# Smaller first transfers, block-wise first products and another order of copies at the start of a macaron block

## The chip, the core and the metric

The kernel runs on one core of a Trainium2 chip. The core has a matrix engine (TensorE, PE in the profile; its weight loads are listed as PEld), VectorE (DVE), ScalarE (ACT), GpSimd (POOL) and SyncE (SP), each with its own instruction stream. They share an on-chip memory of 128 partitions, an accumulator memory in banks of 128 x 512 float32 that TensorE writes, and 16 DMA engines that move data to and from the device's main memory. A transfer is issued by an engine; nearly all of this kernel's are issued by SyncE, in the order of the program.

The metric is the time of one execution on the device in microseconds, the median of several runs.

## The reference

One layer of a decoder with 1024 tokens of width 1024, in float32: a half-step of a SwiGLU feed-forward, a mixer of two branches (dilated window attention and multi-scale pooling), a second half-step, and a final norm. Cut to what matters here:

```python
def rms_norm(x, g):
    xf = x.astype(jnp.float32)
    y = xf * lax.rsqrt(jnp.mean(xf * xf, axis=-1, keepdims=True) + RMS_EPS)
    return (y * g.astype(jnp.float32)).astype(x.dtype)

def swiglu(x, w1, w3, w2):
    return (jax.nn.silu(x @ w1) * (x @ w3)) @ w2

def reference(x, ffn1_norm, ffn1_w1, ffn1_w3, ffn1_w2, ...):
    h = x
    h = h + 0.5 * swiglu(rms_norm(h, ffn1_norm[0]), ffn1_w1[0], ffn1_w3[0], ffn1_w2[0])
    u = rms_norm(h, mix_norm[0])
    ...   # the mixer: h = h + merged @ w_out
    h = h + 0.5 * swiglu(rms_norm(h, ffn2_norm[0]), ffn2_w1[0], ffn2_w3[0], ffn2_w2[0])
    return rms_norm(h, final_norm)
```

The first half-step multiplies the normed x (1024 x 1024) by w1 and w3 (1024 x 2816 each). The change lies in the first few of these products.

## The kernel before

**Numbers.** A float32 operand is split into a rounded high part (made by ScalarE, `AF.Copy` into a type that TensorE multiplies in one pass) and a low part, the rest (made by VectorE or GpSimd as source minus high part). A product of two such operands is three matmuls: high by high, high by low, low by high (`three`). One *product* below is a 128-column piece of a weight over 512 rows of the contraction against 512 tokens: 4 blocks of 128 rows x 3 matmuls = 12 matmuls of 128 x 128 by 128 x 512.

**Seven products for eight.** The multiplications by w1 and w3 are done on 2 x 2 halves (contraction by tokens) with seven products in place of eight. The class `Quad` holds one 128-column piece of w1 (`a`) or w3 (`b`); quads 0 and 1 are `f10a` and `f10b`, quads 2 and 3 `f11a` and `f11b`, quads 4 and 5 `f12a` and `f12b`. Product m of a quad takes a weight operand and one of seven operands made of x:

- `b11` and `b21`: x of the first 512 tokens, rows 0 to 3 and 4 to 7 of the contraction in blocks of 128 (products 1 and 2).
- `b22`, and the sums `t2`, `t3`, `t1`, `t4` (products 3, 6, 7, 5 and 4).

`high(what, k, ...)` and `low(what, k, ...)` make the two parts of block k of such an operand; `operand(n, m)` makes the weight operand of product m of quad n (the high part on ScalarE, line 322; the low part on GpSimd or VectorE, line 325); `run(n, m)` issues the 12 matmuls (line 334), and `out(n, m)` takes the result from its bank. `led` products are product 1 of two later pairs, run ahead because x is still coming in: `led_high`, `led_run` and `led_out`, which copies the bank to the tile `s_f1led` and sends it to main memory.

**Order.** The stretch is written out by hand in the function `begin_up1` (`manual_schedule`): each engine does its instructions in the order in which the lines issue them, and waits on the others only for data and for places. `load_all` issues the transfers in one list on SyncE: x turned so that the contraction lies on partitions (`x_t`, two blocks of 128 rows in one transfer), the first halves of four weights (`raw0` to `raw3`), led weights, and then x by tokens (`row_x`), from which ScalarE takes the mean squares.

ffn1_norm (`gain1`) multiplies x while it is rounded (line 1057 the high part, line 1066 the low one). The root of the mean square is applied later, to the results: `squares_of_x`, `inverses`, `spread` (four transposes by `ident`, line 1115) and `spread_copy` put it into the tile `norm`.

**The first two products.** `run_first` issues them (line 1158) with the weights split in two pieces of 256 columns by `split_high` (ScalarE, line 1144) and `split_low` (GpSimd, line 1148). Thirteen small matmuls on a tile of ones (`idle`, line 1041) stand ahead of them.

## Time and profile before

| | |
|---|---|
| median of 3 runs | 1876.85 us (1876.06 to 1878.15) |
| profiled execution | 1876.94 us, its span 1874.9 us |
| TensorE busy | 1864.6 us (99%), 8690 matmuls |
| VectorE busy | 1369.0 us (73%) |
| ScalarE busy | 767.7 us (41%) |
| GpSimd busy | 782.5 us (42%) |
| first product's first matmul | 6.44 us after the span's start |
| granted TensorE clock, mean | 0.999 |

How to read it: times in a timeline count from the span's start. A timeline row is start, duration, engine, source line, operation, what it writes and reads with the buffer numbers left out, the shapes, the count, and in brackets how long the engine sat idle before it and what ended that. A row with x4 stands for four instructions in a row. The name `x_t` is x as loaded, `xhi_b_f` and `xlo_b_f` the parts of b11, b21 or b22, `xhi_t_f` and `xlo_t_f` those of a t operand, `wc_first` and `wc_f10a` and so on weight operands with both parts, `u_...` a bank, `y_f` and `u_f` results.

### The profile page before, as it was taken

What the parts mean: (1) busy time and instruction counts of PE and PEld (TensorE: products, weight loads), DVE (VectorE), ACT (ScalarE), POOL (GpSimd) and SP (SyncE); (2) the same over time, 40 slices, a digit from 0 to 9 for tenths busy, and PEclk for the clock granted to TensorE, in tenths of its full rate; (3) what the DMA queues carried; (4) which work ended last, traced back from release to release, by engine and by line L of the source; (5) the groups of instructions that cost most, each with busy time, mean ns of one, the idle gap of its engine ahead of it and who ended that gap; (6) DMA issues with size and microseconds to landing.
All of it is one profiled execution on the core that took longest, in us unless ns stands there. A gap on an engine that the chain in (4) does not pass through costs nothing.

```text
span 1874.9 us, 24458 instructions
## 1 busy us (share of the span) xinstructions
PE 1864.6 (99%) x8690; PEld 1546.4 (82%) x8690; DVE 1369.0 (73%) x1972; ACT 767.7 (41%) x1392; POOL 782.5 (42%) x566
## 2 busy tenths in 40 slices
PE   9999999999999999999999999999999999999998
PEld 7888888888888888888888888888888888888887
DVE  7887866668886776658885896888765566577867
ACT  8322323333345643334445762463333333334344
POOL 4554644452222364445554457544333333313221
PEclk9999999999999999999999999999999999999999
DMA  8134324356565435765678868734342233354654
GB/s 327 45 124 148 122 95 151 123 200 210 189 234 197 158 114 204 253 221 185 213 251 327 309 223 296 266 133 180 119 140 85 90 107 121 127 200 158 224 198 146
DMA packets 147473, 338.10 MB, mean 180 GB/s; under 512 B 17944, under 2 KB 39448, under 8 KB 145816
## 3 DMA queue, kind: packets, MB, share of 16 engines
q1 hardware_dynamic: 143608, 325.70, 50.3%
q10 hardware_dynamic: 3744, 10.85, 1.5%
q8 instruction: 68, 1.11, 0.3%
q14 instruction: 53, 0.43, 0.1%
HBM read 235.90 MB, written 100.60 MB: 179 GB/s over the span
## 4 chain that ended last, share of the span: by engine, by line
PE 54%; DVE 3%; ACT 2%; issue 1%; DMA 1%; POOL 1%; ACTq 0%; SPq 0%; DVEq 0%; POOLq 0%
PE u_mixm L334 15%; PE d_f L904 8%; PE wo L2345 4%; PE yp L2087 1%; PE u_f20a L334 1%; PE u_f21b L334 1%; PE u_f20b L334 1%; PE u_f21a L334 1%; PE u_f210b L334 1%; PE u_f210a L334 1%; PE u_f29b L334 1%; PE u_f29a L334 1%; PE u_f28b L334 1%; PE u_f28a L334 1%; PE u_f27b L334 1%
## 5 line engine op out<-in xcount | busy, mean ns | idle before, releaser
L904 PE MATMUL d_f<-bhi_f,ahi_f 128*128 128x512 f32 x616 | 240.2, 390 | 0.0
L904 PE MATMUL d_f<-bhi_f,alo_f 128*128 128x512 f32 x616 | 239.8, 389 | 0.0
L904 PE MATMUL d_f<-blo_f,ahi_f 128*128 128x512 f32 x616 | 239.6, 389 | 0.0
L861 POOL TENSOR_TENSOR alo_f<-g_f,ahi_f 128x512 fp32r<-128x512 f32 x60 | 89.6, 1511 | 266.2 <-ACT ahi_f L857 266.2
L334 PE MATMUL u_mixm<-xhi_t_mix,wc_mixm 128*128 128x512 f32 x608 | 157.3, 391 | 0.1
L904 PEld LDWEIGHTS d_f<-bhi_f,alo_f 128*128 128x128 f32 x616 | 115.6, 188 | 24.5 <-DVE alo_f L861 0.2
L904 PEld LDWEIGHTS d_f<-bhi_f,ahi_f 128*128 128x128 f32 x616 | 115.7, 188 | 24.2 <-ACT h L424 0.5
L904 PEld LDWEIGHTS d_f<-blo_f,ahi_f 128*128 128x128 f32 x616 | 115.7, 188 | 23.7
L334 PEld LDWEIGHTS u_mixm<-xhi_t_mix,wc_mixm 128*128 128x128 f32 x608 | 113.5, 188 | 23.8 <-ACT wc_mixm L322 0.6
L334 PE MATMUL u_mixm<-xhi_b_mix,wc_mixm 128*128 128x512 f32 x456 | 120.3, 391 | 0.0
L325 POOL TENSOR_TENSOR wc_mixm<-s_mixm,wc_mixm 128x512 fp32r<-128x512 f32 x52 | 77.9, 1499 | 99.1 <-ACT wc_mixm L322 88.2
L334 PEld LDWEIGHTS u_mixm<-xhi_b_mix,wc_mixm 128*128 128x128 f32 x456 | 85.0, 188 | 17.2
L322 ACT ACTIVATE wc_mixm<-s_mixm 128x512 fp32r<-128x512 f32 x76 | 47.0, 628 | 110.4 <-DVE s_mixm L378 54.1
L857 ACT ACTIVATE ahi_f<-g_f 128x1024 fp32r<-128x1024 f32 x84 | 81.9, 975 | 7.9 <-DMA g_f<-gs_f 7.9
L334 PE MATMUL u_mixm<-xlo_t_mix,wc_mixm 128*128 128x512 f32 x304 | 81.3, 389 | 0.0
L325 POOL TENSOR_TENSOR wc_mixm<-raw,wc_mixm 128x512 fp32r<-128x512 f32 x41 | 62.3, 1524 | 38.7 <-ACT wc_mixm L322 35.2
L2345 PE MATMUL wo<-w_o,o_hi 128*128 128x512 f32 x224 | 69.3, 390 | 0.0
L646 POOL TENSOR_TENSOR y_f<-y_f,norm_ffn 128x512 f32<-128x512 f32 x35 | 54.4, 1560 | 35.5 <-DVE y_f L627 25.2
L857 ACT ACTIVATE bhi_f<-s_f2w 128x512 fp32r<-128x512 f32 x55 | 32.9, 628 | 86.2 <-DVE s_f2w L879 67.3
L857 ACT ACTIVATE bhi_f<-s_f1w 128x512 fp32r<-128x512 f32 x55 | 33.1, 629 | 83.8 <-DVE s_f1w L879 71.1
L334 PEld LDWEIGHTS u_mixm<-xlo_t_mix,wc_mixm 128*128 128x128 f32 x304 | 57.1, 188 | 11.9
L861 DVE TENSOR_TENSOR alo_f<-g_f,ahi_f 128x1024 fp32r<-128x1024 f32 (+1 forms) x48 | 59.7, 1245 | 7.6 <-ACT ahi_f L857 7.6
(1357 smaller groups left out, 4822.6 us busy)
## 6 DMA issues: line engine op xcount, KB each, us to landing
g_f<-gs_f SPq DMA_DIRECT2D x70, 512.0 KB
gs_f<-y_f SPq DMA_DIRECT2D x88, 256.0 KB
raw<-in_w2a_dram SPq DMA_DIRECT2D x35, 512.0 KB
raw<-in_w2b_dram SPq DMA_DIRECT2D x35, 512.0 KB
gs_f<-gb_f SPq DMA_DIRECT2D x46, 256.0 KB
raw<-in_w1b_dram SPq DMA_DIRECT2D x22, 512.0 KB
raw<-in_w3b_dram SPq DMA_DIRECT2D x22, 512.0 KB
raw<-in_w1a_dram SPq DMA_DIRECT2D x20, 512.0 KB
```

What stands on the lines that cost most here:

```text
L322: ac.activation(w[:, 0], src, AF.Copy)
L325: eng.tensor_tensor(w[:, 1], src, w[:, 0].bitcast(F32), op=OP.subtract)
L334: pe.matmul(p, a, b, start=(start and n == 0), stop=(n == 11), skip_group_check=not start)
L646: gp.tensor_tensor(c, c, self.sv.norm[:, cols], op=OP.mult)
L857: ac.activation(hi[:, c], src, AF.Copy)
L861: eng.tensor_tensor(lo[:, d], src[:, o], hi[:, d].bitcast(F32), op=OP.subtract)
L904: pe.matmul(self.banks[m][t], l, r, start=(first and q == 0), stop=(last and q == 2))
L2087: pe.matmul(p, a, b, start=(j == 0), stop=(j == 11))
L2345: pe.matmul(banks[m][t], l, r, start=(st == 0 and j == 0 and q == 0), stop=(st == 1 and j == 1 and q == 2))
```

## The change

1. x of the first four blocks comes in four transfers of one block each, in place of two of two blocks. The norm's gain, before on ScalarE's queue, is SyncE's second transfer, right behind the first block; the other transfers stand in another order behind it. `ident` goes from ScalarE's queue to SyncE's, behind four of the row transfers.
2. The first two products run block by block of the contraction, both quads' matmuls of one block before the next, with the matmuls that need x's low part last within a block from block 1 on. All of b11's high parts are made by ScalarE (block 1 was made by VectorE).
3. Ten idle matmuls in place of thirteen; the small `less` is computed later.
4. ScalarE's copies stand in another order up to the end of the stretch. The first two `led_out` copies are made by VectorE.

The diff, cut to its core:

```diff
-    nc.scalar.dma_start(gain1, ffn1_norm)
-    nc.scalar.dma_start(ident, c_ident)
...
+        def half_of_features(k):
+            nc.sync.dma_start(xt(0, k), x_t[0, k // 2][:, k % 2])
...
-        features(0, 0)
+        half_of_features(0)
+        nc.sync.dma_start(gain1, ffn1_norm)
         weight(0, LOWS)
+        half_of_features(1)
         weight(1, LOWS)
-        features(0, 1)
+        half_of_features(2)
+        half_of_features(3)
         weight(2, LOWS)
         weight(3, LOWS)
+        led_weight(0)
         features(0, 2)
-        led_weight(0)
+        led_weight(1)
         features(0, 3)
-        led_weight(1)
...
+        nc.sync.dma_start(ident, c_ident)
...
-        for _ in range(13):
+        for _ in range(10):
...
-        def led_out(q):
-            ac.activation(led_in[q], led_p.pop(q), AF.Copy)
+        def led_out(q, eng=ac):
+            if eng is ac:
+                ac.activation(led_in[q], led_p.pop(q), AF.Copy)
+            else:
+                ve.tensor_copy(led_in[q], led_p.pop(q))
...
-        run_first(0, (0, 1), (0, 1, 2))
-        run_first(1, (0, 1), (0, 1, 2))
+        run_first(0, 0, (0, 1, 2))
+        run_first(0, 1, BOTH)
+        run_first(1, 0, (0, 1, 2))
+        run_first(1, 1, BOTH)
+        run_first(0, 1, OTHER)
+        run_first(1, 1, OTHER)
...
         for k in (2, 3):
             high("b11", k, xt(0, k), gain(k))
-        for k in (2, 3):
             low("b11", k, xt(0, k), gain(k))
-        run_first(0, (2, 3), (0, 2, 1))
-        run_first(1, (2, 3), (0, 2, 1))
+            for terms in (BOTH, OTHER):
+                for n in (0, 1):
+                    run_first(n, k, terms)
...
-        led_out(0)
         for k in (2, 3):
             low_b22(k)
+        led_out(0, ve)
+        led_out(1, ve)
...
         inverses(1)
+        out(3, 2)
+        run(4, 1)
+        out(4, 1)
         for k in (0, 1):
             high("t3", k, xt(0, k))
             low("t3", k, xt(0, k))
-        out(3, 2)
         operand(5, 2)
-        run(4, 1)
-
-        out(4, 1)
...
-        operand(0, 7)
         spread_copy(1, p)
-        out(4, 2)
         for k in (2, 3):
             high("t1", k, xt(1, k), gain(k))
             low("t1", k, xt(1, k), gain(k))
+        operand(0, 7)
+        out(4, 2)
```

Here `BOTH` is the terms high by high and low weight by high x, `OTHER` high weight by low x; lists of terms in the old code are in the same numbering.

TensorE at the first products, before (`u_first0` is quad 0's bank, `u_first1` quad 1's; `xhi_b11`, `xlo_b11` x's parts):

```order
L1041 MATMUL idle_246<-ones_73 128x128 x13
L1158 MATMUL u_first0_276<-xhi_b11_f1_128,wc_first0_264 128x512 x2
L1158 MATMUL u_first0_276<-xlo_b11_f1_129,wc_first0_264 128x512 x2
...
L1158 MATMUL u_first1_283<-xlo_b11_f1_129,wc_first1_271 128x512 x2
L1158 MATMUL u_first1_283<-xhi_b11_f1_128,wc_first1_271 128x512 x2
L1158 MATMUL u_first0_276<-xhi_b11_f1_128,wc_first0_264 128x512 x4
```

and with the change:

```order
L1046 MATMUL idle_248<-ones_73 128x128 x10
L1169 MATMUL u_first0_274<-xhi_b11_f1_126,wc_first0_261 128x512
L1169 MATMUL u_first0_274<-xlo_b11_f1_127,wc_first0_261 128x512
L1169 MATMUL u_first0_274<-xhi_b11_f1_126,wc_first0_261 128x512 x3
L1169 MATMUL u_first1_280<-xhi_b11_f1_126,wc_first1_269 128x512
L1169 MATMUL u_first1_280<-xlo_b11_f1_127,wc_first1_269 128x512
L1169 MATMUL u_first1_280<-xhi_b11_f1_126,wc_first1_269 128x512 x3
```

Before, quad 0 took two blocks of x at once; now it takes one block, then the next, and quad 1 follows the same way.

ScalarE between the row squares and t4, before (`xhi_t3`, `xhi_t1`, `xhi_t4` are roundings of x operands, `wc_f10a7` the weight operand of product 7):

```order
L322 ACTIVATE wc_f12a2_551<-raw4_238 128x512
L1057 ACTIVATE xhi_t3_f1_545<-x_t00_138 128x512 x2
L322 ACTIVATE wc_f12b2_581<-raw5_240 128x512
L610 ACTIVATE y_f12_0_597<-u_f12a1_584 128x512
L1057 ACTIVATE xhi_t3_f1_545<-x_t01_139 128x512 x2
...
L1057 ACTIVATE xhi_t1_f1_547<-x_t10_136,gain1_114 128x512 x2
L322 ACTIVATE wc_f10a7_645<-s_f10a3_643 128x512
```

and with the change:

```order
L322 ACTIVATE wc_f12a2_550<-raw4_240 128x512
L610 ACTIVATE y_f12_0_589<-u_f12a1_576 128x512
L1061 ACTIVATE xhi_t3_f1_544<-x_t00_136 128x512 x2
...
L1061 ACTIVATE xhi_t1_f1_546<-x_t11_135,gain1_114 128x512 x2
L322 ACTIVATE wc_f10a7_649<-s_f10a3_647 128x512
L322 ACTIVATE wc_f10a5_678<-s_f10a1_569 128x512
```

The copy of u_f12a moved ahead of t3's roundings, and the copy of the weight of product 7 behind all of t1's; the one of product 5 comes right after it, ahead of t4's.

VectorE around the sum for product 7 (`s_f10a3`), before:

```order
L1064 TENSOR_TENSOR xlo_t3_f1_546<-x_t00_138,xhi_t3_f1_545 128x512 x2
L666 TENSOR_TENSOR y_f11_0_358<-u_f11b1_343,y_f11_0_358 128x512
L1064 TENSOR_TENSOR xlo_t3_f1_546<-x_t01_139,xhi_t3_f1_545 128x512 x2
L1066 SCALAR_TENSOR_TENSOR xlo_t1_f1_548<-x_t10_136,gain1_114,xhi_t1_f1_547 128x512 x2
...
L382 TENSOR_TENSOR s_f10a3_643<-raw0_207,raw6_554 128x512
```

and with the change:

```order
L666 TENSOR_TENSOR y_f11_0_357<-u_f11b1_342,y_f11_0_357 128x512
L1068 TENSOR_TENSOR xlo_t3_f1_545<-x_t00_136,xhi_t3_f1_544 128x512 x2
L1068 TENSOR_TENSOR xlo_t3_f1_545<-x_t01_137,xhi_t3_f1_544 128x512 x2
L1070 SCALAR_TENSOR_TENSOR xlo_t1_f1_547<-x_t10_134,gain1_114,xhi_t1_f1_546 128x512 x2
...
L1070 SCALAR_TENSOR_TENSOR xlo_t1_f1_547<-x_t11_135,gain1_114,xhi_t1_f1_546 128x512 x2
L382 TENSOR_TENSOR s_f10a3_647<-raw0_206,raw6_553 128x512
```

L666 moved ahead of t3's low parts, and the second two of t1's low parts ahead of L382.

More of the change, by code (lines that the diff above doesn't have):

```diff
@@ L1039, in begin_up1 @@
         idle = bank("mm", "idle")
-        for _ in range(13):
+        for _ in range(10):
             pe.matmul(idle[:, :P], ones, ones, start=True, stop=True)
         ve.memset(fours, -0.5)
-        ve.tensor_scalar(less, gain1, -1.0, None, op0=OP.mult)
         pairs = [Pair(sv1, j, sums, True, (lambda n: u2_last[:, :HALF]) if j == 2 else None) for j in range(3)]
@@ L1148, in split_low, with run_first @@
             gp.tensor_tensor(w[:, 1, c], quads[n].a[0][:, c], w[:, 0, c].bitcast(F32), op=OP.subtract)
-        def run_first(n, ks, terms):
+        FRONT, BACK = slice(0, 2 * P), slice(2 * P, HALF)
+        BOTH, OTHER = (0, 2), (1,)
+        steps = {n: 0 for n in (0, 1)}
+        def run_first(n, k, terms):
             if n not in banks:
@@ L1153, in run_first @@
             w, (hi, lo) = first[n], X["b11"]
+            r = slice(k * P, (k + 1) * P)
             for i in terms:
-                for k in ks:
-                    r = slice(k * P, (k + 1) * P)
-                    a, b = three((w[:, 0, r], w[:, 1, r]), (hi[:, k, :], lo[:, k, :]))[i]
-                    pe.matmul(banks[n], a, b, start=(k == 0 and i == 0), stop=(k == 3 and i == terms[-1]))
-        FRONT, BACK = slice(0, 2 * P), slice(2 * P, HALF)
+                a, b = three((w[:, 0, r], w[:, 1, r]), (hi[:, k, :], lo[:, k, :]))[i]
+                steps[n] += 1
+                pe.matmul(banks[n], a, b, start=(steps[n] == 1), stop=(steps[n] == 12))
         high("b11", 0, xt(0, 0), gain(0))
-        high("b11", 1, xt(0, 1), gain(1), ve)
         split_high(0, FRONT)
+        low("b11", 0, xt(0, 0), gain(0))
+        split_low(0, FRONT)
         split_high(0, BACK)
-        split_low(0, FRONT)
-        low("b11", 0, xt(0, 0), gain(0))
+        high("b11", 1, xt(0, 1), gain(1))
         low("b11", 1, xt(0, 1), gain(1))
@@ L1172, in begin_up1 @@
         split_low(1, BACK)
-        run_first(0, (0, 1), (0, 1, 2))
-        run_first(1, (0, 1), (0, 1, 2))
+        run_first(0, 0, (0, 1, 2))
[4 more added lines that the diff above has]
+        run_first(1, 1, OTHER)
+        ve.tensor_scalar(less, gain1, -1.0, None, op0=OP.mult)
         def high_b21(k):
@@ L1193, in begin_up1 @@
             high("b11", k, xt(0, k), gain(k))
-        for k in (2, 3):
             low("b11", k, xt(0, k), gain(k))
-        run_first(0, (2, 3), (0, 2, 1))
-        run_first(1, (2, 3), (0, 2, 1))
+            for terms in (BOTH, OTHER):
+                for n in (0, 1):
+                    run_first(n, k, terms)
         operand(2, 1)
         operand(3, 1)
+        led_high(0)
+        out(0, 1)
         high_b21(4)
         low_b21(4)
-        out(0, 1)
         high_b21(5)
-        led_high(0)
         low_b21(5)
@@ L1208, in begin_up1 @@
         out(1, 1)
+        led_high(1)
         high_b21(6)
-        led_high(1)
         high_b21(7)
@@ L1252, in begin_up1 @@
         sums_of(1)
+        led_out(2)
         high("t2", 1, t2[1])
@@ L1255, in begin_up1 @@
             low("t2", k, t2[k])
-        led_out(2)
         operand(2, 2)
@@ L1264, in begin_up1 @@
         sums_of(2)
-        high("t2", 2, t2[2])
         half_roots(0)
@@ L1270, in begin_up1 @@
         spread_copy(0, p)
+        high("t2", 2, t2[2])
         out(0, 2)
@@ L1295, in begin_up1 @@
             low("t3", k, xt(0, k))
-        out(3, 2)
         operand(5, 2)
-        run(4, 1)
-        out(4, 1)
+        run(5, 1)
         for k in (2, 3):
@@ L1303, in begin_up1 @@
             low("t3", k, xt(0, k))
+        out(5, 1)
         operand(0, 6)
-        run(5, 1)
-        out(5, 1)
         for k in (0, 1):
```

3 lines of the change are left out of this document (1 added, 2 removed).

## The prediction

> **What bounds the kernel now.** I read the page first, then the waits of TensorE (PE), then the timeline of the first 67 us, where the whole change lies.
>
> ```profile
> span 1874.9 us, 24458 instructions
> PE 1864.6 (99%) x8690; PEld 1546.4 (82%) x8690; DVE 1369.0 (73%) x1972; ACT 767.7 (41%) x1392; POOL 782.5 (42%) x566
> PE idle L1041 <- DVE fours L1042: 1.1, 1, 1.1
> PE u_first L1158 <- ACT wc_first L1144: 0.7, 1, 0.7
> PE u_f12a L334 <- ACT y_f L610: 0.4, 1, 0.4
> ...
> PE u_f10a L334 <- ACT wc_f10a L322: 0.3, 1, 0.3
> ```
>
> TensorE is busy for 99% of the span, and its waits in the whole trace come to about 3 us. So the kernel ends when TensorE has streamed its matmuls. This change moves no matmul out of the program; it can only remove idle time or add it. Busy hides something, though: the first 4.65 us are matmuls on ones that warm the engine up, and matmul ends overlap. Starts tell more:
>
> ```profile
> 1.05 4.65 PE L1041 MATMUL idle<-ones 128*128 128x128 f32 x26 [1.05 <-DVE fours L1042]
> 4.58 0.72 ACT L1057 ACTIVATE xhi_b_f<-x_t,gain 128x512 fp32r<-128x512 f32 x1 [1.43 <-DMA gain<-in_ffn_norm_dram]
> 5.34 1.41 DVE L1066 SCALAR_TENSOR_TENSOR xlo_b_f<-x_t,gain,xhi_b_f 128x512 fp32r<-128x512 f32 x2 [0.20 <-ACT xhi_b_f L1057]
> 5.97 1.59 ACT L1144 ACTIVATE wc_first<-raw 128x256 fp32r<-128x256 f32 x4 [0.67 <-DMA raw<-in_w1a_dram]
> 6.44 0.73 PE L1158 MATMUL u_first<-xhi_b_f,wc_first 128*128 128x512 f32 x2 [0.74 <-ACT wc_first L1144]
> 6.46 2.98 POOL L1148 TENSOR_TENSOR wc_first<-raw,wc_first 128x256 fp32r<-128x256 f32 x4 [6.02 <-ACT wc_first L1144]
> 8.34 1.34 ACT L1057 ACTIVATE xhi_b_f<-x_t,gain 128x512 fp32r<-128x512 f32 x2 [0.78 <-DMA x_t<-in_x_t_dram]
> 10.98 0.72 ACT L1057 ACTIVATE xhi_b_f<-x_t,gain 128x512 fp32r<-128x512 f32 x1 [0.26 <-DMA x_t<-in_x_t_dram]
> 12.43 1.07 PE L334 MATMUL u_f11a<-xhi_b_f,wc_f11a 128*128 128x512 f32 x4
> 15.15 1.07 PE L334 MATMUL u_f11b<-xhi_b_f,wc_f11b 128*128 128x512 f32 x4
> 34.19 0.60 PE L1115 MATMUL norm<-ident,roots 128*128 128x128 f32 x4
> 34.54 1.17 PE L334 MATMUL u_f11a<-xhi_b_f,wc_f11a 128*128 128x512 f32 x4
> ```
>
> A product is 12 matmuls. From u_f11a to u_f11b is 15.15 - 12.43 = 2.72 us, or 0.227 us a matmul. The eight products between 12.43 and 34.19 take 21.76 = 8 x 2.72: there TensorE is dense. Before that the 24 matmuls of the first two products need 24 x 0.227 = 5.44 us and have 12.43 - 6.44 = 5.99. So the start can give back the wait for the first matmul and 0.55 us of small stalls. The next looseness is later:
>
> ```profile
> 42.81 1.07 PE L334 MATMUL u_f12b<-xhi_b_f,wc_f12b 128*128 128x512 f32 x4
> 45.47 0.58 ACT L610 ACTIVATE y_f<-u_f12a 128x512 f32<-128x512 f32 x1
> 46.10 1.19 PE L334 MATMUL u_f12a<-xhi_b_f,wc_f12a 128*128 128x512 f32 x4 [0.40 <-ACT y_f L610]
> 52.14 1.07 PE L334 MATMUL u_f10a<-xhi_t_f,wc_f10a 128*128 128x512 f32 x4
> 57.33 0.61 ACT L322 ACTIVATE wc_f10a<-s_f10a 128x512 fp32r<-128x512 f32 x1
> 57.99 1.19 PE L334 MATMUL u_f10a<-xhi_t_f,wc_f10a 128*128 128x512 f32 x4 [0.25 <-ACT wc_f10a L322]
> 66.56 1.19 PE L334 MATMUL u_f10b<-xhi_t_f,wc_f10b 128*128 128x512 f32 x4
> ```
>
> From 42.81 to 66.56 lie eight products and four small transposes (0.35 us, as from 34.19 to 34.54): 21.76 + 0.35 = 22.11 us against 23.75. So 1.64 us are lost there: 46.10 - 45.53 = 0.57 before the second u_f12a, 57.99 - 57.58 = 0.41 before the third f10a product, and 0.66 in smaller pieces.
>
> **The change, part by part: the start.** What sets the first products is when bytes land, on one queue in the order of issue.
>
> ```profile
> x_t<-in_x_t_dram SPq DMA_DIRECT2D x8, 512.0 KB
> raw<-in_w1a_dram SPq DMA_DIRECT2D x2, 256.0 KB
> ident<-in_c_ident_dram ACTq DMA_DIRECT2D x1, 64.0 KB
> gain<-in_ffn_norm_dram ACTq DMA_DIRECT2D x1, 4.0 KB
> ```
>
> Add up bytes against the waits above. Blocks 0 and 1 of x with gain and ident, 580 KB, are there at 4.58; the first weight half makes 836 KB at 5.97; the second, blocks 2 and 3 make 1604 KB at 8.34; 2628 KB at 10.98. The slopes are 184, 324 and 388 KB per us. In the new order (block 0, gain, weight 0, block 1, weight 1, block 2, block 3) I read arrivals off that line: weight 0 completes 516 KB, at about 4.4; block 1 772 KB, 5.6; weight 1 1028 KB, 5.97 + 192/324 = 6.56; block 2 1284 KB, 7.35; block 3 1540 KB, 8.14. Ident's 64 KB leave the front; it is issued as the 24th transfer and its first reader starts at 34.19. The three added issues cost nothing on the path: SyncE issues in some 0.4 us, while 256 KB take 0.66 us even at 388 KB per us.
>
> Block 0 is rounded by ScalarE (0.72), then the first half of the weight's columns: the first matmul comes near 5.2, over a microsecond ahead of 6.44. That isn't yet time gained, since each product now stops for the next block. The last such stop is weight 1: from 6.56, ScalarE's copy takes 1.59/4 = 0.40, GpSimd's rest 2.98/4 = 0.75; with 0.05 for each signal the eighth matmul, the one that needs that rest, starts at 7.8. The 17 from there on are dense: blocks 2 and 3 land at 7.35 and 8.14, and 0.72 of ScalarE and about 0.75 of VectorE (1.41/2 = 0.71 each at L1066) end before their matmuls come up at 8.9 and 10.3. So u_f11a starts at 7.8 + 17 x 0.227 = 11.65, not 12.43: **0.78 us**. Bounds: never a stop from 5.2 on, 5.2 + 5.44 = 10.64, or 1.79 gained; transfers at 184 KB per us throughout, weight 1 at 4.0 + 772/184 = 8.2 and u_f11a at 13.3, or 0.85 lost. I take 0.78 because weight 1 lies between two measured points.
>
> The idle matmuls fall from 13 to 10.
>
> ```profile
> L1041 PE MATMUL idle<-ones 128*128 128x128 f32 x8 | 1.8, 397 | 0.0
> L1041 PE MATMUL idle<-ones 128*128 128x128 f32 x11 | 1.4, 275 | 0.0
> 4.50:5.00 0.50, 0.50 (x7) 0.50 (x7) 0.42 (x2) 0.42 (x1) 0.00 (x0) 1.00 0.86 285
> ```
>
> The first row is the stretch 3.0 to 4.2, the second 4.5 to 8.3: each record shortens from 397 to 275 ns, so the engine comes up to speed at about 4.3. At seven records per 0.5 us the six records (three matmuls) less are 0.43 us, and the ten end at 5.27, still past that point and no later than the first product wants to start. I put the cost at nothing; were the slow pace of 1.05 to 4.3 to last as long again, it would be 3.25 x (1 - 275/397) = 1.0 us.
>
> **The order of copies, 20 to 67 us.** Two led copies go from ScalarE to VectorE, where the chain already waits:
>
> ```profile
> 26.16 1.41 DVE L1078 SCALAR_TENSOR_TENSOR x_t<-x_t,less,x_t 128x512 f32<-128x512 f32 x1 [1.40 <-ACT s_f1led L1097]
> ```
>
> VectorE stood 1.40 us there for just such a copy. Two of its own at about 0.7 us fill that wait, so its sums start where they did: nothing, cover included; without the wait, 1.4 us on VectorE. The copy of u_f12a moves ahead of t3's rounding, so the 0.57 us at 46.10 should go. The weight copy for the third f10a product now precedes t4's four roundings, so the 0.41 us at 57.99 goes too. Of the 0.66 in small pieces I count half, 0.33. Against that stands one delay, in the s_f10a step (L382), which needs to be rounded for the second f10a product:
>
> ```profile
> 44.56 1.98 DVE L1064 TENSOR_TENSOR xlo_t_f<-x_t,xhi_t_f 128x512 fp32r<-128x512 f32 x2 [1.39 <-ACT xhi_t_f L1057]
> 46.46 0.68 DVE L666 TENSOR_TENSOR y_f<-u_f11b,y_f 128x512 f32<-128x512 f32 x1
> 47.06 3.26 DVE L1064 TENSOR_TENSOR xlo_t_f<-x_t,xhi_t_f 128x512 fp32r<-128x512 f32 x2
> 50.24 1.40 DVE L1066 SCALAR_TENSOR_TENSOR xlo_t_f<-x_t,gain,xhi_t_f 128x512 fp32r<-128x512 f32 x2
> 51.71 0.68 DVE L382 TENSOR_TENSOR s_f10a<-raw,raw 128x512 f32<-128x512 f32 x1
> 52.48 0.63 ACT L322 ACTIVATE wc_f10a<-s_f10a 128x512 fp32r<-128x512 f32 x1 [3.16 <-DVE s_f10a L382]
> ```
>
> The new order puts two more of t1's low parts (1.40) ahead of L382, and L666 (47.06 - 46.46 = 0.60) out into the wait before 44.56. ScalarE's chain before t3 runs some 0.7 us earlier with TensorE, but now does 0.58 of copy there first, so t3 starts as before. L382 ends at 51.71 + 0.68 + 1.40 - 0.60 = 53.19, its rounding (0.63 and 0.05 of signal) at 53.87. TensorE wants it at 11.65 + 21.76 + 0.35 + 5 x 2.72 + 0.35 + 2 x 2.72 = 53.15: a new stall of **0.7 us**. Bounds: 0, if the slow pair at 47.06 (1.63 us each, beside 0.70 at 50.24) runs free; 2.5, if t1's added pair runs as slowly as that one (1.86 more). I take 0.7, the rows as they are. What is late next is hidden: the third f10a product's weight is copied right behind.
>
> **Sum** on the profiled run of 1876.94 us (span 1874.9 and 2.04 around it): -0.78 - 0.57 - 0.41 - 0.33 + 0.7 = -1.39, or 1875.55. The median shown, 1876.85, is 0.09 lower, so **1875.5**.
>
> "DMA: Bandwidth & Descriptors" of the Trainium skill, section Bandwidth, asks for transfers of 1 MiB or more, and has 64 KB at 32% and 1 MB at 78% of peak. That speaks against halving x's transfers to 256 KB. Here the row of 256 KB pieces in flight together shows 388 KB per us, and the slow 184 at the very front; by the page the front would stay slow, and the sum would be nearer the second rival's -0.4 than -1.4.
>
> **Rivals.** *Everything dense*: no stops from 5.2 on and VectorE in time: -1.79 - 1.64 = -3.4, 1873.4. For it: the late waits each have a named copy that moves. Against: weight 1 can't land early by any row. *The small transfers are no quicker*, 184 KB per us at the front: u_f11a at 13.3, +0.85; then L382 is no stall, and -1.31 stays: -0.4, 1876.4. For it: the first slope; against: the next two. *VectorE becomes the bound* (slower): the led copies add 1.4 behind a wait that stays, and t1's added pair takes 3.26, not 1.40. L382 ends at 53.19 + 1.4 + 1.86 = 56.4, its product starts at 57.1 against 54.86: +2.2, less 0.7 of the late gains, +1.5, 1878.4. It decides once L382 ends after 54.2 (54.86 less 0.63). For it: VectorE has little idle from 17 to 52 us; against: the 1.40 and 1.39 of waits.
>
> **How the numbers follow.** Forecast 0.62, dense 0.15, no quicker 0.13, VectorE 0.10. The forecast's own range is 1874.4 to 1876.4. The range 1873.0 to 1877.6 takes in dense nearly whole and half of the VectorE case, and the 2 us by which the three runs shown differ. About 0.2%, 3.75 us, is what a measurement tells from no change: below 1873.1 lies only an upper fringe of dense with luck, 0.05; above 1880.6 only a doubled VectorE case, 0.03; within, 0.92.
>
> **What would show it.** Right: first product near 5.2, u_f11a at 11.3 to 12.0, no wait on y_f L610, a short wait on the second f10a weight near 53, and nothing changed after 67 us but an earlier clock. Wrong: u_f11a after 12.4 (transfers), or L382 ending after 54.2 (VectorE), or a wait after 67 us that the trace of before doesn't have.

## The result, and the profile after

The changed kernel takes 1880.2 us (median; 1879.95 to 1881.9) where the kernel before takes 1876.9 on the same chips: a ratio of 1.0019, 95% interval [1.0012, 1.0026]. It is slower by 3.3 us, where 1.4 faster was forecast, and lies outside the forecast's range. The page and the waits of TensorE after the change:

```profile
span 1878.5 us, 24451 instructions
PE 1866.2 (99%) x8684; PEld 1547.0 (82%) x8684; DVE 1371.4 (73%) x1973; ACT 767.4 (41%) x1391; POOL 779.4 (41%) x566
PE u_first L1169 <- ACT xhi_b_f L1061: 1.4, 1, 1.4
...
PE u_f10a L334 <- DVE y_f L627: 0.8, 1, 0.8
PE u_f10a L334 <- ACT wc_f10a L322: 0.7, 1, 0.7
...
PE u_f12a L334 <- ACT y_f L610: 0.2, 1, 0.2
```

The waits that the change should have removed have shrunk or gone (0.7 ahead of the first matmul, u_f12a 0.4 to 0.2, the third f10a product), and three have come: 1.4 in the first products, and 0.7 and 0.8 in `f10a`. In time order, TensorE's rows that answer to those of before:

```profile
5.14 0.50 PE L1169 MATMUL u_first<-xhi_b_f,wc_first 128*128 128x512 f32 x1
7.84 0.50 PE L1169 MATMUL u_first<-xhi_b_f,wc_first 128*128 128x512 f32 x1 [1.38 <-ACT xhi_b_f L1061]
14.36 1.07 PE L334 MATMUL u_f11a<-xhi_b_f,wc_f11a 128*128 128x512 f32 x4
57.84 1.19 PE L334 MATMUL u_f10a<-xhi_t_f,wc_f10a 128*128 128x512 f32 x4 [0.73 <-ACT wc_f10a L322]
67.07 1.17 PE L334 MATMUL u_f10a<-xhi_b_f,wc_f10a 128*128 128x512 f32 x4 [0.77 <-DVE y_f L627]
70.00 1.19 PE L334 MATMUL u_f10b<-xhi_t_f,wc_f10b 128*128 128x512 f32 x4
```

`u_f11a` starts 1.93 us later than before (12.43), `f10b` 3.44 later (66.56); behind it the distance hardly grows (span +3.6). So all is lost in the first 70 us, 1.9 before `u_f11a` and 1.5 after it. This is one execution, 0.8 above the median (1880.96), and its start holds a stretch at half clock (last section); a usual execution loses less before `u_f11a`. ScalarE's timeline shows the start:

```profile
3.79 0.72 ACT L1061 ACTIVATE xhi_b_f<-x_t,gain 128x512 fp32r<-128x512 f32 x1 [1.56 <-DMA gain<-in_ffn_norm_dram]
4.67 0.72 ACT L1151 ACTIVATE wc_first<-raw 128x256 fp32r<-128x256 f32 x2 [0.17 <-DMA raw<-in_w1a_dram]
7.06 0.72 ACT L1061 ACTIVATE xhi_b_f<-x_t,gain 128x512 fp32r<-128x512 f32 x1 [1.67 <-DMA x_t<-in_x_t_dram]
9.46 0.72 ACT L1061 ACTIVATE xhi_b_f<-x_t,gain 128x512 fp32r<-128x512 f32 x1 [0.40 <-DMA x_t<-in_x_t_dram]
10.82 0.63 ACT L322 ACTIVATE wc_f11b<-raw 128x512 fp32r<-128x512 f32 x1
14.38 0.63 ACT L1093 ACTIVATE wc_led<-s_f1led 128x512 fp32r<-128x512 f32 x1 [2.93 <-PE u_first L1169]
15.40 1.32 ACT L1061 ACTIVATE xhi_b_f<-x_t,gain 128x512 fp32r<-128x512 f32 x2
```

Block 0 and the first weight come early, as forecast (3.79 and 4.67), but block 1 is taken up only at 7.06 where 5.6 was expected. (It varies: with the same list of transfers, profiles of the variants below have it at 5.45 to 7.54.) And further on ScalarE stands 2.93 us in front of the first led rounding. That instruction was moved ahead of blocks 4 and 5, and it waits for TensorE: converted weights share four places (`bufs=4`), the two first weights and `f11a`, `f11b` have them, and the led weight is the fifth; it gets the first one's place when the first product is done. So block 4, rounded at 10.98 before, is rounded at 15.40. VectorE carries that on:

```profile
28.45 1.86 DVE L1082 SCALAR_TENSOR_TENSOR x_t<-x_t,less,x_t 128x512 f32<-128x512 f32 x1
35.21 1.85 DVE L1082 SCALAR_TENSOR_TENSOR x_t<-x_t,less,x_t 128x512 f32<-128x512 f32 x1
39.48 0.68 DVE L619 TENSOR_TENSOR y_f<-u_first,norm_ffn 128x512 f32<-128x512 f32 x1
56.39 0.68 DVE L382 TENSOR_TENSOR s_f10a<-raw,raw 128x512 f32<-128x512 f32 x1
58.19 1.52 DVE L387 TENSOR_TENSOR s_f10a<-raw,s_f10a 128x512 f32<-128x512 f32 x1
59.63 4.69 DVE L1068 TENSOR_TENSOR xlo_t_f<-x_t,xhi_t_f 128x512 fp32r<-128x512 f32 x4
66.23 0.69 DVE L627 TENSOR_TENSOR y_f<-u_f10a,y_f 128x512 f32<-128x512 f32 x1
```

Before, the sum at 35.21 (L1078 there) took 0.75, L619 stood at 35.82, L382 at 51.71, and t4's four low parts took 2.49 us ahead of L612 and L387; now they stand behind L387 and take 4.69. L627, which product 3 of `f10a` waits for, is behind all of it.

### The profile page after: what moved, and what is told of

The parts are those of the page before. It is cut to its first block, busy times and chain, and to the rows that moved or that the text cites. A ratio compares the mean times of both kernels' runs of the same rounds, so it can differ in the third digit from the quotient of the medians.

```text
span 1878.5 us, 24451 instructions
## 1 busy us (share of the span) xinstructions
PE 1866.2 (99%) x8684; PEld 1547.0 (82%) x8684; DVE 1371.4 (73%) x1973; ACT 767.4 (41%) x1391; POOL 779.4 (41%) x566
## 4 chain that ended last, share of the span: by engine, by line
PE 58%; DVE 1%; ACT 1%; DMA 0%; issue 0%; POOL 0%; ACTq 0%; SPq 0%; DVEq 0%
PE u_mixm L334 15%; PE d_f L904 11%; PE wo L2359 4%; PE yp L2101 1%; PE u_f20a L334 1%; PE u_f21b L334 1%; PE u_f20b L334 1%; PE u_f21a L334 1%; PE u_f210b L334 1%; PE u_f210a L334 1%; PE u_f29b L334 1%; PE u_f29a L334 1%; PE u_f28b L334 1%; PE u_f28a L334 1%; PE u_f27b L334 1%; PE u_f27a L334 1%
## 5 line engine op out<-in xcount | busy, mean ns | idle before, releaser
L334 PEld LDWEIGHTS u_mixm<-xlo_t_mix,wc_mixm 128*128 128x128 f32 x304 | 57.1, 188 | 12.0
```

The lines of the kernel that those rows point to most:

```text
L334: pe.matmul(p, a, b, start=(start and n == 0), stop=(n == 11), skip_group_check=not start)
```

## The experiments

All medians stand beside the kernel before on the same chip (1876.9 to 1877.1); ratios are with 95% intervals. "L619" is the normalisation of `u_first` on VectorE (35.82 before), "f10b" the start of that product (66.56 before); times of both are from one profile of each kernel. `f10a`'s products run in the order 6, 7, 5, 4, 3, so "the third f10a product" is product 5. A cause that hides another, so that undoing the other shows nothing, is called a cover.

A profile is of one execution, which lay between 1.0 us below (new copies) and 1.3 above (the last of the account) its kernel's median, and an interval reaches some 1.7 us to either side. So rows tell what waits for what, medians what it costs, and differences of some tenths between two variants are not settled. From f10b to the end of the span all 18 profiles take 1808.2 to 1809.8 us: what differs lies ahead of it.

### Which half of the change

**The start of before with the new order of copies.**

```diff
 (begin_up1 up to the first products as before; from "operand(2, 1)" on as changed)
+            else:
+                ve.tensor_copy(led_in[q], led_p.pop(q))
```

> The kernel before up to the end of the first two products, with the changed order of copies behind them (and VectorE's two led copies). Theory 'VectorE' (the copies' order itself costs: s_f10a at L382 behind two more low parts, and the bank of the third product freed late): u_f11a at 12.43 as before, product 7 of f10a stalls 0.6 to 0.9 us, product 3 about 0.8, and the kernel is slower than before by 1.2 to 1.6 us, about 1878.3. Rival 'start' (the order only hurts because the start came late): no stall over 0.3 us there, and the time within 0.5 of 1876.9 or below it.

Measured: 1878.7, ratio 1.0009 [1.0000, 1.0019]. `u_f12a` comes 0.51 earlier without a wait, as forecast, then product 7 waits 0.74 and product 3 0.75; L619 at 36.87, f10b at 67.39.

**The changed start with the copies of before.**

> The changed kernel up to the end of the first two products, with the order of copies of before behind them. Theory 'two causes that add': u_f11a at about 14.4, the later stalls as in the kernel before (1.6 us lost between 42.8 and 66.6, no more), and slower than before by 1.8 to 2.1 us, about 1878.8. Rival 'one cause' (the late start is what disturbs the copies): the stalls at the second f10a product and the third one appear here too, and the time is 1879.8 or more.

Measured: 1878.2, ratio 1.0007 [0.9997, 1.0016], where 1878.8 was expected. `u_f11a` is only 0.38 late (12.81; 14.4 expected), but block 4 is rounded at 12.98 instead of 10.98 (ScalarE waits 1.33 for its transfer), and `u_f12a` then waits 1.35 for its copy. The copies alone cost 1.8 and the start alone 1.3 (its interval contains no change); both together cost 3.3. That fits a sum, in which more than half comes with the new order of copies on the old list of transfers.

### The idle matmuls and the clock

**The kernel before with ten idle matmuls; the changed one with 23.**

```diff
-        for _ in range(13):
+        for _ in range(10):        # the other: range(23), in the changed kernel
```

> The kernel before with 10 idle matmuls in place of 13, nothing else. Theory 'clock by the idle matmuls': the idle ones end at 5.3 instead of 5.7, TensorE has 0.4 us less work ahead of its first product at 6.44, and if that is enough to halve the clock, it reads 0.5 for 3.4 us in the first 12 us and u_f11a starts 1.3 to 1.7 us later. Theory 'clock by the gap' (it is the 1.4 us without work at 6.5 to 7.8 and the single matmuls around it that do it): the clock stays 1.0, u_f11a at 12.4, the time within 0.4 of 1876.9.

> The changed kernel with 23 idle matmuls in place of 10; they end near 7.2 us instead of 5.3. In the changed kernel TensorE's granted clock reads 0.50 from 8.2 to 11.7 us. Theory 'clock' (three real matmuls between 5.3 and 7.8 us are too little work, and the clock is halved for one stretch after it): the clock stays 1.0, the 17 matmuls from the eighth on run at 0.227 us, u_f11a starts at 12.7 to 13.1 instead of 14.36, and the time falls by 1.3 to 1.6 us, to about 1878.7. Rival 'transfers' (block 1 of x lands at 7.04 us, and that alone sets everything behind it): u_f11a stays within 0.3 of 14.36 and the time within 0.4 of 1880.2.

Measured: 1877.2, ratio 1.0000 [0.9991, 1.0010], and 1880.8, ratio 1.0019 [1.0009, 1.0028]. Three idle matmuls less cost nothing. Twenty-three, which leave no gap, hold the clock at 1.0, but start the first product at 8.67, so that `u_f11a` stands at 14.23, no earlier than in the changed kernel. Nothing is won, and both theories missed; by itself this doesn't clear the clock. Two runs further down do: with the first product finished first, and with the old last stretch, `u_f11a` stands at 12.47 and 12.64 at full clock, and the kernels are still 3.1 to 3.2 us slower.

### What holds ScalarE at the start

**The led roundings back behind blocks 4 and 5; the old list of transfers; x's blocks 4 and 5, and 6 and 7, each ahead of a led weight as before** (the last on the changed start with the copies of before).

```diff
-        led_high(0)
-        out(0, 1)
         high_b21(4)
         low_b21(4)
+        out(0, 1)
         high_b21(5)
+        led_high(0)
 ...                               # led_high(1) likewise behind high_b21(6)
```

> The changed kernel with the roundings of the first two led weights (L1093) back behind x's blocks 4 and 5, and 4 to 6, in ScalarE's order; nothing else. Theory 'place': in the changed kernel the first led rounding waits 2.93 us for one of the four places of a converted weight and holds block 4 up to 15.40; ScalarE then runs 3.6 to 4.4 us late up to 48. Then block 4 is rounded at about 13.0 (when it lands), the first rounding of t3 starts near 46, not 48.03, the wait of product 7 of f10a (0.73) goes and half of that of product 3 (0.77): the median falls by 0.7 to 1.3 us, to about 1879.2. Rival 'start': the loss is set by the first two products' late end (14.36 against 12.43) and VectorE's own order alone; ScalarE has slack: t3 moves but the late products stay, 1880.2.

> The changed kernel with the list of transfers of before (x in pairs of blocks, gain and ident on ScalarE's queue); products by single blocks and the new order of copies stay. Theory 'chain': TensorE's start doesn't matter, what counts is when block 4 is rounded on ScalarE, since the VectorE work behind it runs without a gap to the third f10a product. With the old list block 4 lands before 11 and is rounded by 13.0 at the latest (behind the first led weight, which waits for the end of the first product); the row squares start near 23.0, the normalisation of u_first (L619) near 36.9, as with the new copies alone, and f10b starts near 67.4 (66.56 before, 70.00 changed): 1878.7 us, 1.5 less than the changed kernel. Rival 'copies': the new order of copies costs the 3.3 whatever lands when, 1880.2. Open beside it: the time outside the span (2.45 in all kernels with the new start and the new copies, 2.0 in the others): if it belongs to the list of transfers, it falls to 2.0.

> The changed start with the copies of before (u_f11a at 12.81, ScalarE 1.34 late from block 4 on, 1878.2 us), now with x's blocks 4 and 5, and 6 and 7, ahead of the first and second led weight on the DMA queue, as before the change. Theory 'queue': the start's 1.3 us come from block 4 landing 2 us later behind the led weight (rounded at 12.98, before 10.98): block 4 is rounded near 11.2, u_f12a is copied on time, its wait falls from 1.35 to about 0.5, and the median is 1877.2 (only the 0.4 of u_f11a is left). Rival 'small pieces': the halves of 256 KB themselves slow the queue; block 4 lands as late, near 12.5, and the median stays near 1878.2.

Measured: 1880.3, ratio 1.0017 [1.0008, 1.0026]; 1879.4, 1.0013 [1.0004, 1.0022]; 1878.2, 1.0006 [0.9998, 1.0015]. Nothing, 0.8, and nothing came back: the theory of one late place missed, and so did the one of block 4 behind the led weight in the queue. ScalarE's rows say why. With the led roundings back, it now waits for the transfer:

```profile
12.54 0.72 ACT L1061 ACTIVATE xhi_b_f<-x_t,gain 128x512 fp32r<-128x512 f32 x1 [1.33 <-DMA x_t<-in_x_t_dram]
```

With the old list the transfer is there, and it waits for the place:

```profile
13.65 0.63 ACT L1088 ACTIVATE wc_led<-s_f1led 128x512 fp32r<-128x512 f32 x1 [3.34 <-PE u_first L1164]
```

Either alone keeps block 4 back to 12.5 or later. Moving x ahead in the new list helps little (12.44 against 12.98), because the whole front of the new list is slower. The windows 0 to 7 and 7 to 11 us of the kernel before, and then of the changed one (behind the length stand the busy time of TensorE's matmuls and weight loads, VectorE, ScalarE and GpSimd; the last two columns are the share of the DMA engines and GB/s):

```profile
0.00:7.00 7.00, 5.21 (x28) 4.94 (x29) 2.16 (x7) 3.10 (x6) 0.74 (x5) 1.00 0.71 223
7.00:11.00 4.00, 4.00 (x17) 2.70 (x16) 1.55 (x2) 2.96 (x7) 3.16 (x5) 1.00 1.02 395
```

```profile
0.00:7.00 7.00, 5.32 (x23) 4.65 (x23) 0.94 (x4) 2.93 (x5) 1.63 (x6) 1.00 0.68 184
7.00:11.00 4.00, 3.16 (x8) 2.36 (x9) 3.18 (x4) 3.50 (x7) 1.81 (x3) 0.66 0.95 350
```

The transfers of the first 7 us, of the kernel before and of the changed one:

```profile
DMA packets 837, 1.56 MB, mean 223 GB/s; under 512 B 213, under 2 KB 341, under 8 KB 837
```

```profile
DMA packets 844, 1.29 MB, mean 184 GB/s; under 512 B 218, under 2 KB 218, under 8 KB 844
```

By 11 us 2.69 MB have come (7 x 184 + 4 x 350) where it was 3.14 before: 0.45 MB, 1.1 us at 395 GB/s. That holds beyond these two: the seven profiles with the new list have 2.55 to 2.82 MB by 11 us, the eleven with the old one 3.10 to 3.21. In the first 7 us as many packets were handled as before (844 and 837) with less in them (1.29 MB against 1.56). That points at the halved transfers, but the list differs also in its order and in gain and ident, and these were not tried apart. The transfer of blocks 4 and 5 is also issued later, 1.06 us in these rows of SyncE, before and after:

```profile
4.57 0.33 SPq L994 DMA_DIRECT2D x_t<-in_x_t_dram  x1
```

```profile
5.63 0.65 SPq L992 DMA_DIRECT2D x_t<-in_x_t_dram  x1
```

With x ahead of the led weight it is issued at 4.96, and block 4 is still rounded only at 12.44; so the late issue alone isn't the cause.

**Both of the first two undone together.**

> The changed kernel with both things undone that can make block 4's rounding late on ScalarE: the old list of transfers (block 4 lands before 11) and the first two led roundings back behind blocks 4 and 5 (no wait for a weight's place ahead of block 4). Undone alone, the one gave 1880.3 and the other 1879.4. Theory 'two covers': each delay alone is as long as both, so only together they free ScalarE: block 4 is rounded by 11.2, row squares begin near 22.7, VectorE's L619 near 36.9 at most (one meeting with GpSimd's subtraction may remain), f10b near 67.4: 1878.2 to 1878.7, as the new copies alone. Rival 'products': the products by single blocks keep the first product open to the end of the start, and something else waits for it; 1879.4 as with the list alone.

Measured: 1879.2, ratio 1.0011 [1.0002, 1.0019]; L619 at 37.79, f10b at 68.32. Better than the led roundings back alone by 1.1, but by only 0.2 than the old list alone: there is a third cover.

```profile
10.85 0.72 ACT L1056 ACTIVATE xhi_b_f<-x_t,gain 128x512 fp32r<-128x512 f32 x1 [0.26 <-DMA x_t<-in_x_t_dram]
13.32 0.60 ACT L610 ACTIVATE y_f<-u_first 128x512 f32<-128x512 f32 x1 [1.74 <-PE u_first L1164]
13.81 0.71 ACT L1056 ACTIVATE xhi_b_f<-x_t,gain 128x512 fp32r<-128x512 f32 x1
```

Block 4 is on time, but behind it in ScalarE's order stands the copy of the first product's bank, and blocks 5 to 7 behind that. Before, the first product was finished 6 matmuls (1.36 us) ahead of the second; run block by block in turns it ends one matmul (0.23) ahead of it.

**The first product finished before the second, alone.**

```diff
-            for terms in (BOTH, OTHER):
-                for n in (0, 1):
-                    run_first(n, k, terms)
+        for n in (0, 1):
+            for k in (2, 3):
+                run_first(n, k, (0, 2, 1))
```

> The changed kernel with that one line alone (over blocks 2 and 3 the first product is finished before the second goes on). Theory 'three covers': the led rounding's wait for the first product's place ends about 1.1 us earlier, near 12.0 to 12.4 instead of 12.7 to 14.4, and then block 4's landing near 12.5 holds ScalarE for itself: gain 0.2 to 0.8, 1879.4 to 1880.0. Rival 'the open first product is the one cause at the start': 1.5 and more come back, 1878.7 or less.

Measured: 1880.1, ratio 1.0017 [1.0008, 1.0026]: 0.1 came back, less than either theory gave. Yet here ScalarE is on time: `u_f11a` stands at 12.47, its first row square at 22.80 (22.68 before). What is late next is the second half of a weight. ScalarE, and then VectorE, of this kernel:

```profile
28.64 0.63 ACT L322 ACTIVATE wc_f10b<-raw 128x512 fp32r<-128x512 f32 x1 [1.10 <-DMA raw<-in_w3a_dram]
29.18 1.04 ACT L1111 ACTIVATE row_x<-row_x 128x1024 f32<-128x1024 f32 x1
```

```profile
30.34 0.32 DVE L1115 TENSOR_SCALAR means<-means 128x4 f32<-128x4 f32 x1 [0.89 <-ACT row_x L1111]
34.04 1.85 DVE L1082 SCALAR_TENSOR_TENSOR x_t<-x_t,less,x_t 128x512 f32<-128x512 f32 x1
```

In the new order of copies, the copy of `wc_f10b` stands ahead of the fourth row square, and it waits for a transfer; VectorE's `means` (28.93 before) wait for that square. Then comes a sum that takes 1.85 us, and L619 is at 38.30, 2.5 late, with a punctual start.

### The sum that takes 1.85

**One swap on ScalarE, in the start of before with the new copies.**

```diff
+        led_out(3)
         operand(2, 2)
         run(0, 2)
 
-        led_out(3)
```

> The start of before with the new order of copies (1878.7 us), with one swap on ScalarE: the fourth led copy goes ahead of the rounding of f11a's weight, so that GpSimd's subtraction for that weight starts 0.5 us later (near 33.1, not 32.61, when VectorE's third sum L1078 also begins). Theory 'port': the 1.86 us of that sum (0.75 elsewhere) come from a GpSimd instruction that begins no later than it; now VectorE is first, the sum takes 0.75, L619 starts at 35.8 to 36.0, and the median falls by up to 1.0 to 1877.7. Rival 'the sum is long for itself' (its PSUM source or its place): it takes 1.86 again, L619 stays at 36.9, 1878.7.

Measured: 1877.4, ratio 1.0002 [0.9993, 1.0011]: 1.3 us less by one swap, more than the 1.0 expected. (In its profile L619 stands at 36.70, not at 36.0 as expected: in this execution the start was 1.2 late, and the sum short all the same.) Without the swap, VectorE and GpSimd:

```profile
32.60 1.86 DVE L1078 SCALAR_TENSOR_TENSOR x_t<-x_t,less,x_t 128x512 f32<-128x512 f32 x1
```

```profile
32.61 1.30 POOL L325 TENSOR_TENSOR wc_f11a<-raw,wc_f11a 128x512 fp32r<-128x512 f32 x1 [1.85 <-ACT wc_f11a L322]
```

With it:

```profile
33.32 0.75 DVE L1078 SCALAR_TENSOR_TENSOR x_t<-x_t,less,x_t 128x512 f32<-128x512 f32 x1
34.11 0.75 DVE L1081 SCALAR_TENSOR_TENSOR x_t<-x_t,less,x_t 128x512 f32<-128x512 f32 x1
```

```profile
33.82 1.40 POOL L325 TENSOR_TENSOR wc_f11a<-raw,wc_f11a 128x512 fp32r<-128x512 f32 x1 [2.34 <-ACT wc_f11a L322]
```

Where both begin together, VectorE's sum is held up by 1.1 us and ends at 34.46, 0.55 behind the subtraction (33.91); where it began half a microsecond earlier, it isn't, and L1081 isn't either, though it runs beside the subtraction from 34.11 on. L1078 reads two tiles of the on-chip memory; L1081 reads one, and one bank of the matmuls' results.

The Trainium skill bears this out: "GPSIMD Engine Reference", section Key points, says that GpSimd shares its memory interfaces with VectorE, and contends with VectorE's instructions that have two inputs there; "Trainium Architecture — The Big Picture", section What this means for kernel authors, calls it an exclusive lock. The trace agrees: 1.86 against 0.75 for the instruction with two such inputs, which ends behind the whole subtraction and not at half its pace, and no difference for L1081.

**The same kernel with the first two led copies back on ScalarE.**

```diff
-        led_out(0, ve)
-        led_out(1, ve)
+        led_out(0)                 # and led_out(1) behind squares_of_x(3)
```

> The start of before with the new order of copies (1878.7 us, L619 of u_first at 36.87, before 35.82), now with the first two led copies on ScalarE where they were, and with them the second high weight's copy (wc_f10b) back behind the fourth row square. Theory 'VectorE's led copies cost': with them back the shift is gone with which GpSimd's wc_f11a subtraction began together with VectorE's third sum (1.86 against 0.75); L619 is back at 35.8 to 36.0, product 7 of f10a (0.74) doesn't wait, the sum ahead of the third block's product (0.75) is 1 us earlier, and f10b starts near 66.3: 1876.6. Rival 'last stretch': the order from t3 on (the next sums ahead of t4's low parts) makes product 7 and product 3 wait whatever came before; f10b near 67.4, 1878.5.

Measured: 1878.0, ratio 1.0006 [0.9997, 1.0015]; 0.6 better, not 2. The theory missed in its mechanism: the sum is long again, since both engines again begin together (32.36 and 32.36), L619 is at 36.62, and product 7 and product 3 wait 0.6 and 0.8.

### The last stretch

**The last stretch in the old order.**

```diff
-        spread_copy(1, p)
-        for k in (2, 3): ...       # high and low of t1
         operand(0, 7)
+        spread_copy(1, p)
         out(4, 2)
+        for k in (2, 3): ...
```

> The changed kernel with the last stretch in the old order: the s_f10a step (L382) and the normalisation of u_f12a (L619) stand again ahead of t1's second pair, which also puts the next product's sum (L612, L387) back behind t4's four low parts on VectorE; nothing else. Theory 'order on VectorE': t4's low parts no longer fall beside GpSimd's wc_f10a subtractions; they take 2.5 us, not 4.69, L382 ends one pair (1.4) earlier, so product 7 (0.73) and product 3 (0.77) don't wait: the median falls by 1.5 us to 1878.7, and f10b starts near 68.5, not 70.00. Rival 'ScalarE': t3 comes 4 us late from ScalarE and both waits stay in the new order too, 1880.2. Rival 'contention anyway': t4's low parts fall beside GpSimd's work all the same and take 4.5 us; product 3 waits, product 7 doesn't, 1879.5.

Measured: 1880.2, ratio 1.0015 [1.0006, 1.0023]: no gain. t4's low parts take 2.49 again and products 7 and 3 no longer wait, but then:

```profile
12.64 1.07 PE L334 MATMUL u_f11a<-xhi_b_f,wc_f11a 128*128 128x512 f32 x4
...
60.05 1.19 PE L334 MATMUL u_f10a<-xhi_t_f,wc_f10a 128*128 128x512 f32 x4 [1.51 <-ACT wc_f10a L322]
```

This is the row that changed my view most. TensorE is 0.21 late at `u_f11a`, as good as on time, and yet the third f10a product starts at 60.05 where it was 57.99: 2.06 late. What sets that product is the chain over ScalarE and VectorE (blocks 4 to 7, the sums, L619 at 38.19, t3, L382, this weight), not TensorE; its wait of 0.25 in the profile of before was the tip of it.

### The whole account

**Four things undone or swapped: list, led roundings, the order around `wc_f10b` and `wc_f11a` (here the fourth led copy goes ahead of the weight's, which is so in neither kernel), the last stretch; and then the first product finished first as well.**

> As the one before, and two more things undone or swapped: the fourth row square back ahead of the second high weight's copy and the fourth led copy ahead of f11a's weight (so that GpSimd's subtraction no longer begins with VectorE's third sum), and the last stretch from s_f10a (L382) on in the old order. Of the change there stay the products by single blocks, fewer idle matmuls, two led copies on VectorE and the copies of u_f12a and u_f12b ahead of t3. Theory 'account complete': what is undone is all that costs; L619 at 35.8 to 36.7, no wait at product 7 and product 3, f10b at 66.3 to 66.8: 1876.7 to 1877.2, as before the change. Rival 'products by blocks cost': 0.5 to 1.5 remain, 1877.7 or more.

> As the kernel with four things undone (1878.6 us; u_first ends near 13.0, its copy L610 at 13.19 after a wait of 1.52, and behind it x's block 5 at 13.68, before 12.09), with one more line: over blocks 2 and 3 the first product is finished before the second goes on, as before the change, so that it ends 5 matmuls (1.1 us) earlier at the same end of both. Theory 'third cover': the copy of u_first starts near 12.1, row squares near 22.8, L619 of u_first near 36.0, f10b 0.9 to 1.2 earlier than 67.60, near 66.5: 1877.0 to 1877.7. Rival: TensorE's later start (0.79 at u_f11a) sets the norm and with it L619; nothing moves, 1878.6.

Measured: 1878.6, ratio 1.0007 [0.9998, 1.0016], and 1877.7, ratio 1.0004 [0.9995, 1.0012]. The first missed its 1877.2; its ScalarE waits 1.52 for the open first product. The second, at the edge of the 1877.0 to 1877.7 expected, has that closed, and what stays of the change (products by blocks up to block 1, ten idle matmuls, two led copies on VectorE, two copies ahead of t3, and two smaller swaps of ScalarE's order) can no longer be told from the kernel before. Some 0.8 us lie inside that interval and are not explained.

### A version meant to beat both

**The kernel before with the copies of u_f12a and u_f12b ahead of t3; and with t1's last two high parts ahead of the waiting weight copy as well.**

```diff
+        out(3, 2)
+        run(4, 1)
+        out(4, 1)
         for k in (0, 1): ...       # t3
-        out(3, 2)
...
+            high("t1", k, xt(1, k), gain(k))     # k = 2, 3
         operand(0, 7)
```

> The kernel before with one part of the change alone: the copies of u_f12a and u_f12b (L610, L666) ahead of t3's roundings, 42 to 48 us; start, led copies, weights and the last stretch as before. Theory: the wait of 0.40 at 46.10 and with it 0.57 us go, t3 on ScalarE starts no later than 0.6, and VectorE's L382 keeps its place ahead of t1's second pair, so product 7 doesn't wait more than 0.1: the median falls by 0.5 us to 1876.4. Rival 'no gap to give': ScalarE's 0.58 of copy ahead of t3 delays L382 by 0.6 and product 7 waits 0.6 instead: 1876.9, nothing gained.

> A version meant to beat both: the kernel before with the copies of u_f12a and u_f12b ahead of t3 (alone 1876.9), and also the roundings of t1's second pair on ScalarE (1.33) ahead of the weight copy that waits 2.89 us for L382; VectorE's order stays. Theory 'chain': ScalarE does them in its wait, VectorE doesn't wait 1.77 for them, the roundings of t4 and the third f10a product's weight come 1.3 earlier (55.7, not 57.05), TensorE runs without a stop from 45.5 on, f10b starts near 65.0 (66.56 before) and the median is 1875.4. Rival 'another wait takes its place': the step L382 ends no earlier, GpSimd's share of the weights or the sum L627 becomes the last, f10b near 66.2, 1876.7.

Measured: 1876.9, ratio 0.9998 [0.9989, 1.0007], and 1876.4, ratio 0.9997 [0.9988, 1.0005]. The first moves the wait from `u_f12a` (gone, 0.58 earlier) to the third f10a product (0.69), not to product 7 as expected, and the 1876.4 forecast didn't come; f10b gains 0.27. The second removes that one, and product 3 waits 0.55 for L627 instead:

```profile
63.08 1.17 PE L334 MATMUL u_f10a<-xhi_b_f,wc_f10a 128*128 128x512 f32 x4 [0.55 <-DVE y_f L627]
```

Its f10b is at 66.02, 0.54 earlier than before, and the median 0.6 lower, where 1875.4 was expected; the interval doesn't tell that from no change.

## Why the prediction was wrong, by its steps

- **What bounds the kernel.** "The kernel ends when TensorE has streamed its matmuls" is right for the 1800 us behind; for the first 70 it was the step that failed. I took TensorE's waits and gaps (0.4 and 0.25 among them) as all that could be won, and 0.7 at L382 as all that could be lost. What sets those products is a chain from the transfers over ScalarE and VectorE, which wait for each other (in the rows of before, VectorE 1.40 and 1.39 us for ScalarE, ScalarE 3.16 us for L382); the experiment with the old last stretch shows the third f10a product 2.06 late with TensorE only 0.21 late.
- **The start, 0.78 gained.** Wrong in sign. The line of arrivals was drawn through bytes alone. In this profile weight 0 was taken up at 4.67 (4.4 expected), block 1 at 7.06 (5.6), block 3 at 9.46 (8.14): 256 KB in 2.4 us between the first two. `u_f11a` stood at 14.36 here, at 14.23 with 23 idle matmuls, and at 12.47 to 13.21 in the other five variants with the new list; the bound on the slow side, 13.3, held for these five and not for the first two. Both signs that the prediction named came: `u_f11a` after 12.4, and L382 ending after 54.2. The Trainium skill's "DMA: Bandwidth & Descriptors", section Bandwidth, which was weighed there as speaking against halved transfers, had the direction right: 184 against 223 GB/s in the first 7 us, though no run halved the transfers and changed nothing else.
- **What the start is worth.** Not costed at all: that the pieces issued behind (blocks 4 to 7, the row and weight halves) come later too, by 1.1 us of bytes, and that the three added issues, put at nothing, are part of what has blocks 4 and 5 issued 1.06 later; that a first product which stays open holds back its copy and what ScalarE has behind it; and that a led rounding moved ahead needs a place. The place could be read beforehand, from `bufs=4` and a count of five.
- **Idle matmuls, nothing.** Right: 1.0000.
- **Two led copies on VectorE, nothing.** The cover was there: VectorE fills its wait. But the price came from the neighbours: the order of ScalarE's row squares, and GpSimd's subtraction starting together with a sum (1.1).
- **u_f12a 0.57 and the third product 0.41.** The first was there to 0.06 (0.51 to 0.58 in four kernels with the start of before); the second wait went too in the changed kernel. They weren't gains, since the next product waited for the same chain.
- **L382, 0.7 lost.** Mis-sized: it ended at 57.07 where 53.19 was forecast and where 54.2 was named as the point from which VectorE decides. The rival "VectorE becomes the bound" had the place and nearly its time (56.4, the product at 57.1; measured 57.84), not the reason, and 0.10 of the chance. With the start of before (the new copies alone) product 7 waited 0.74, near the 0.7 of the forecast, but by luck: L382 ended 1.3 later than forecast there too, with 1.1 of it from the sum that took 1.86.
- **Not seen in the diff.** The sums for the next product (L612, L387) stand ahead of t4's low parts on VectorE in the changed program. That follows from moving the normalisation of u_f12a (L619) behind t1's second pair; the lines themselves were not touched.

## What to carry to other kernels

A wait of a few tenths on the busiest engine can be the tip of a chain on other engines; before pricing a change by that engine's rows, follow what releases the wait back to the transfers and look for an experiment where the busy engine is on time and the wait is there all the same. Where three things each hold the same instruction back, undoing one shows nothing: read from the trace what it waits for then, and undo that as well. When an instruction is moved ahead, count the places that it needs and name what stands behind it in its queue.
